# Gates made ahead and kept in DRAM, and up-projections moved past a triangular solve, in a five-branch decoder trunk

## The chip, the cores and the metric

The kernel runs on one core of a Trainium2 chip. The metric is the device time of one execution in microseconds (us). Names of engines: PE is TensorE (its weight loads are PEld), DVE is VectorE, ACT is ScalarE, POOL is GpSimd, SP is SyncE, whose queue issues nearly all DMAs.

## What is computed

One layer: a normalised input, one combined projection, four causal token mixers and one cross-attention, each with an up-projection and a merge gate of its own, and an output projection. SEQ is 2048, D_MODEL 1024, a branch is 512 wide, and everything is float32.

```python
h = rms_norm(x, norm_g[l])
p = h @ w_in[l]
(ret_q, ..., mem_q, gates) = split_cols(p, IN_SIZES)
o_ret = retention_branch(ret_q, ret_k, ret_v, positions) * silu(ret_g)
...                                  # o_gla, o_ssd, o_rwkv, o_mem in the same way
g = sigmoid(gates).reshape(b, t, N_BRANCHES, d)
merged = g[:, :, 0] * (o_ret @ w_up_ret[l])
for i in range(1, N_BRANCHES):
    merged = merged + g[:, :, i] * (o_i @ w_up_i[l])   # gla, ssd, rwkv, mem
x = x + merged @ w_out[l]
```

The gates need only the projection of `h`, so a gate can be made at any time of its pass. An up-projection needs the output `o` of its branch.

## The kernel before

The sequence is worked through in four passes of 512 tokens (`run`, the loop over `sc`). A pass does its branches in the order mem, retention, RWKV-7, SSD, GLA. While a branch is worked on, the gates and up-projections of the branch before it are fed in as units of work.

**Units.** `gate_units` makes eight pairs for a branch: `gate(d)` multiplies the normalised input by one 128-column block of gate weights (`proj`: 24 matmuls of 512 columns, since each float32 product is made of three parts) and ACT takes the tanh of it into an SBUF tile; `up(d)` multiplies the branch's output by a block of up weights (`mm3`: 12 matmuls, 6 for mem), DVE adds 1 to the tanh and multiplies (`stt`, line 302), and POOL or DVE adds the product to `merged[d]` (L1382). `inter` puts a branch's units in the order g0 g1 u0 g2 u1 ... g7 u6 u7, and they go to the list `self.fq`. Every `self.fill(n)` in a branch takes n units off that list. How many at which place is written out in `K.FILL`.

**Around the change.** Retention uses 8 of mem's 16 units, so when RWKV begins the list holds 8 of mem, 16 of retention and 4 output gates of RWKV (`rw_g`). RWKV has three parts. `rwkv_prep` makes its inputs (DVE, ACT and POOL do most of it). `rwkv_sys` inverts 64 triangular blocks: DVE solves by 31 pairs of a multiply and a row sum (L1196 and L1198), transposes twice (L1201 and L1203), ACT and POOL copy (L1208), and then PE does eight short groups, `lower(i)` and `corner(i)`, with copies between them. `fill(12)` stands behind the solve's lines and `fill(3)` ahead of `lower(0)`, so 15 units stand ahead of it; `lower(0)` is moreover tied to come after the last of them (`after=self.last`). `rwkv_chain` is a recurrence of eight chunks, with 13 units left for it. GLA comes last: its eight gates run one after the other behind it, then its eight ups, each with a slice of the next pass's input (`xhat_units`).

**Order.** The program's order is not the issue order. Behind `start` a planner orders each engine's instructions, SP's DMAs among them, ahead of time: an instruction that the planner takes to be ready may be moved ahead of earlier ones that are not, and its idea of the time is its own. On the chip each engine then runs its list strictly in that order. SBUF tiles named `s` come from one pool of 42 (`NS`), gate weights from four buffers (`wt`), the accumulators `acc` are three PSUM banks. Weights are split into two parts in the first pass and kept in DRAM (`kw`); later passes load them from there, 1 MB for a gate and 512 KB for an up (256 KB for mem).

Of the kernel before, what the change touches and what calls it, by code (L numbers as in the profile page):

```python
# [17 lines left out]
P = 128  # L18
# [126 lines left out]
class K:  # L145
# [131 lines left out]
    def nm(self, s):  # L277
        self.n += 1
        return f"{s}_{self.n}"

    NS = 42

    FILL = {"mem": (2, 0, 2, 2, 1, 1, 3, 3), "ret": (1, 3, 0), "late": (0, 0, 0, 0), "sys": (12, 3), "chain":
            (2, 3, 2, 1, 1, 2, 4, 3), "norm": 0, "ssd": (6, 0, 3, 4, 4), "gla": (3, 1, 2, 3, 1), "eng": (0, 1,
# [876 lines left out]
    def rwkv_sys(self, AR, KB):  # L1161
# [69 lines left out]
        for i in range(4):  # L1231
            nxt = lower(i + 1) if i < 3 else None
            corner(i, *z)
            z = nxt
# [103 lines left out]
    def rwkv(self, sc):  # L1338
        sg = []
        g = [lambda p=p: sg.append(self.silu2(self.proj(f"rw_g{p}"))) for p in range(4)]  # L1340
        self.fq += g
        wa = self.shift(12)
        self.nc.scalar.activation(wa[0:64, :], wa[0:64, :], AF.Tanh)
        AR, KB, gC = self.rwkv_prep(wa, range(4))
        Tt = self.rwkv_sys(AR, KB)
        BV = self.rwkv_chain(AR, KB, gC, Tt)
        self.fill(99)

        self.misc(sc)
        self.bm = [self.conv(sc, 4 + g) for g in range(2)]  # L1350
        return self.rwkv_fin(sc, BV, sg)


    def gate_units(self, key, o, eng=None):
        nc = self.nc
        nk = BRK[key]
        first = self.merged is None
        if first:
            self.merged = [None] * KT
        merged = self.merged  # L1360
        us = []
        for d in range(KT):
            th = []

            def gate(d=d, th=th):
                g = self.proj(f"gate{8 * BR[key] + d}")
                t = self.s()
                self.act(t, g, AF.Tanh, scale=0.5)
                th.append(t)

            def up(d=d, th=th):
                w = self.load_w(("wu_" + key, d), nk)
                ps = self.ps("acc")
                self.mm3(ps, w, lambda k: o[k], nk)
                t = th[0]
                if first:
                    m = self.xp.tile([P, T], F32, tag=f"mg{d}", name=self.nm("mg"))
                    merged[d] = m
                    self.stt(m, t, 1.0, ps, ALU.add, ALU.mult)
                else:  # L1380
                    self.stt(t, t, 1.0, ps, ALU.add, ALU.mult)
                    (eng or self.pick({"ret": 0, "rwkv": 1, "ssd": 2, "gla": 3}[key])).tensor_tensor(  # L1382
                        merged[d], merged[d], t, ALU.add)

            us.append((gate, up))
        return us

    @staticmethod
    def inter(us):

        g, u = [a for a, _ in us], [b for _, b in us]
        out = g[:2]
        for i in range(len(us)):
            out.append(u[i])
# [132 lines left out]
    def run(self):  # L1527
        for sc in range(self.nsc):
            last = sc + 1 == self.nsc
            self.merged = None  # L1530
            o = self.mem(sc)
            self.fill(99)
            for key, nxt in (("mem", "ret"), ("ret", "rwkv"), ("rwkv", "ssd"), ("ssd", "gla")):
                us = self.gate_units(key, o)
                self.fq += self.inter(us)
                if nxt == "ssd" and not last:
# [6 lines left out]
            self.bg = []  # L1543
            us = self.gate_units("gla", o, self.nc.vector if last else None)
            for gate, _ in us:
                gate()
            if not last:
                self.xh, xu = self.xhat_units(sc + 1, rs[0])
            hl = []
            for k in range(KT):  # L1550
                if not last:
                    xu[k]()
                us[k][1]()
            for k in range(KT):
# [85 lines left out]
```

## Time and profile before

| | us |
|---|---|
| runs: median of three | 3657.2 |
| runs: lowest and highest | 3652.63, 3668.01 |
| the profiled execution: its own time | 3662.73 |
| the profiled execution: span from first to last instruction | 3660.9 |
| PE busy in that span | 3462.5 (95%) |
| DVE, ACT and POOL busy | 1981.0, 983.9, 898.7 |
| mean granted clock of PE, as a share of full speed | 0.963 |

The triangular solve of the four passes ends near 400, 1336, 2211 and 3088 us, so a pass takes some 877 us; the first one starts behind the setup and also splits the weights. Matmuls are pipelined, so a busy PE need not be PE at its peak; the step from one start to the next tells the pace. The granted clock has two levels, 1.0 (2.4 GHz) and 0.5 (1.2 GHz). In the views, a number in square brackets behind an instruction is the time that its engine stood idle ahead of it, and what ended that.

### The profile page before, as it was taken

The page shows a single profiled execution, that of the slowest core. Times are in us where ns is not written, and L with a number is a line of the kernel's source. Part 1 is how long each engine was busy: PE and PEld are TensorE (multiplying, and loading weights), DVE is VectorE, ACT ScalarE, POOL GpSimd, SP SyncE. Part 2 cuts the span into 40 slices and gives each one's busy share as a digit, 9 for nine tenths or more (in the row PEclk, how much of TensorE's full clock was granted, in tenths as well). Part 3 has the DMA queues.
Part 4 walks back from the last instruction along what each step waited for, and adds up shares of the span by engine and source line. Part 5 has one row for each costly group of instructions (what it writes and reads, how often), then busy time and mean ns, then how long its engine had stood idle before and what let it go on. Part 6 is the DMA issues. An engine that isn't in the chain of part 4 may idle for free.

```text
span 3660.9 us, 51745 instructions
## 1 busy us (share of the span) xinstructions
PE 3462.5 (95%) x20368; PEld 2770.1 (76%) x20368; DVE 1981.0 (54%) x3189; ACT 983.9 (27%) x1796; POOL 898.7 (25%) x919
## 2 busy tenths in 40 slices
PE   7988898999899999999999998999999998999998
PEld 5766667777778677888887776778887877778887
DVE  6377557644454865662353785664345377464243
ACT  4243224342321321322131221222122132131212
POOL 3556425455421410211101231021100132020110
PEclk8988899999999989999999998999999999999999
DMA  6655535676765543545565553345465554344555
GB/s 201 229 191 188 176 120 202 212 253 218 267 212 164 159 136 113 178 150 172 170 221 175 153 172 116 124 152 184 161 215 184 169 158 147 111 151 149 170 171 191
DMA packets 226531, 639.59 MB, mean 175 GB/s; under 512 B 25184, under 2 KB 46192, under 8 KB 226288
## 3 DMA queue, kind: packets, MB, share of 16 engines
q1 hardware_dynamic: 225856, 635.76, 52.3%
q8 instruction: 161, 2.64, 0.3%
q14 instruction: 82, 0.67, 0.1%
q10 hardware_dynamic: 432, 0.52, 0.0%
HBM read 486.76 MB, written 145.23 MB: 173 GB/s over the span
## 4 chain that ended last, share of the span: by engine, by line
PE 53%; DVE 15%; issue 2%; ACT 2%; DMA 2%; POOL 0%; SPq 0%; DVEq 0%; POOLq 0%; ACTq 0%
PE acc L305 42%; DVE s L302 6%; PE br L305 6%; PE y L305 4%; DVE s L299 3%; DVE blk L299 2%; DVE blk L1198 1%; ACT s L296 1%; PE br L317 1%; DMA wt<-kw 1%; DMA s<-vtd 1%; DVE s L329 0%; DMA s<-in_xT_dram 0%; ACT blk L1182 0%; DVE s L339 0%
## 5 line engine op out<-in xcount | busy, mean ns | idle before, releaser
L305 PE MATMUL acc<-xhi,wt 128*128 128x512 f32 x5632 | 1836.1, 400 | 47.1 <-DVE s L299 15.2
L305 PEld LDWEIGHTS acc<-xhi,wt 128*128 128x128 f32 x5632 | 1075.5, 192 | 297.2 <-ACT s L296 20.8
L305 PE MATMUL acc<-xlo,wt 128*128 128x512 f32 x2816 | 1123.5, 399 | 2.3 <-DVE xlo L1518 1.5
L305 PEld LDWEIGHTS acc<-xlo,wt 128*128 128x128 f32 x2816 | 540.1, 192 | 115.5 <-issue 3.0
L305 PE MATMUL acc<-s,wt 128*128 128x512 f32 (+1 forms) x2448 | 600.9, 395 | 15.5 <-ACT wt L378 7.6
L305 PEld LDWEIGHTS acc<-s,wt 128*128 128x128 f32 x2448 | 455.8, 191 | 115.4 <-ACT wt L378 14.3
L302 DVE SCALAR_TENSOR_TENSOR s<-s,acc 128x512 f32<-128x512 f32 x192 | 131.4, 684 | 630.0 <-PE acc L305 348.6
L379 POOL TENSOR_TENSOR wt<-wr,wt 128x512 fp32r<-128x512 f32 (+1 forms) x256 | 354.7, 1391 | 406.6 <-ACT wt L378 391.8
L302 DVE SCALAR_TENSOR_TENSOR s<-s,s 128x512 f32<-128x512 f32 (+1 forms) x458 | 361.1, 792 | 30.9 <-ACT s L296 18.8
L379 POOL TENSOR_TENSOR s<-s,s 128x512 fp32r<-128x512 f32 x120 | 159.2, 1335 | 887.3 <-ACT s L378 758.3
L296 ACT ACTIVATE s<-acc 128x512 f32<-128x512 f32 x232 | 136.8, 596 | 725.1 <-PE acc L305 723.8
L1382 POOL TENSOR_TENSOR mg<-mg,s 128x512 f32<-128x512 f32 x64 | 87.4, 1366 | 576.5 <-DVE s L302 576.2
L378 ACT CAST wt<-wr 128x512 fp32r<-128x512 f32 (+1 forms) x256 | 155.5, 611 | 268.3 <-PE acc L305 132.9
L305 PE MATMUL br<-s,s 64*64 64x64 f32 (+6 forms) x2432 | 213.2, 279 | 15.2 <-DMA s<-vtd 4.8
L305 PEld LDWEIGHTS br<-s,s 64*64 64x64 f32 (+3 forms) x2432 | 165.1, 167 | 67.7 <-issue 40.8
L296 ACT ACTIVATE s<-s 128x512 f32<-128x512 f32 (+1 forms) x204 | 119.3, 610 | 298.6 <-DVE s L299 121.9
L378 ACT CAST s<-s 128x512 fp32r<-128x512 f32 x182 | 112.8, 620 | 300.9 <-DVE s L302 270.7
L299 DVE TENSOR_TENSOR s<-s 128x512 f32<-128x512 f32 (+1 forms) x167 | 149.2, 898 | 6.1
L305 PE MATMUL y<-s,s 128*64 128x64 f32 (+4 forms) x2112 | 138.0, 255 | 9.2 <-DVE s L299 6.7
L305 PEld LDWEIGHTS y<-s,s 128*64 128x64 f32 (+2 forms) x2112 | 113.5, 152 | 39.8 <-DVE s L299 12.5
L299 DVE TENSOR_TENSOR s<-s,s 128x512 f32<-128x512 f32 (+2 forms) x154 | 118.2, 793 | 41.2 <-ACT s L296 39.7
L317 PE MATMUL br<-cst,s 128*128 128x128 f32 x484 | 82.9, 296 | 49.5 <-DVE s L302 38.1
(218 smaller groups left out, 3247.3 us busy)
## 6 DMA issues: line engine op xcount, KB each, us to landing
wt<-kw SPq DMA_DIRECT2D x712, 512.0 KB, 3.3
kw<-wt SPq DMA_DIRECT2D x240, 512.0 KB, 3.1
wr<-in_wg_dram SPq DMA_DIRECT2D x176, 256.0 KB, 3.8
s<-in_xT_dram SPq DMA_DIRECT2D x88, 256.0 KB, 4.9
out_dram<-s SPq DMA_DIRECT2D x24, 256.0 KB, 2.5
wt<-kw SPq DMA_DIRECT2D x24, 256.0 KB, 3.1
s<-s SPq DMA_DIRECT2D x64, 64.0 KB, 2.0
bvd<-s SPq DMA_DIRECT2D x16, 256.0 KB, 2.6
```

The source lines that it names most:

```text
L296: self.nc.scalar.activation(out, in_, f, bias=bias, scale=scale, **kw)
L299: self.nc.vector.tensor_tensor(out, a, b, op)
L302: self.nc.vector.scalar_tensor_tensor(out, a, s, b, op0, op1)
L305: i = self.nc.tensor.matmul(out, lhsT=lhsT, rhs=rhs, start=start, stop=stop)
L317: self.nc.tensor.transpose(out, in_, self.c["ident"])
L378: self.nc.scalar.copy(hi, src)
L379: (eng or self.nc.gpsimd).tensor_tensor(lo, src, hi.bitcast(F32), ALU.subtract)
L1198: nc.vector.tensor_reduce(X[:, s_, s_ + 1:], pv, AX.X, ALU.add)
L1382: (eng or self.pick({"ret": 0, "rwkv": 1, "ssd": 2, "gla": 3}[key])).tensor_tensor(merged[d], merged[d], t, ALU.add)
```

## The change

The gates of all branches but mem become units of their own (`gates` with `far=True`): the tanh is stored to a DRAM tile as soon as it is made, and `up(d)` loads it again, the load for `up(d + 1)` being issued in `up(d)` (and the one for d = 0 there as well). Five gates (`EARLY`) of RWKV, SSD and GLA join the list of the branch before; three stay in the list of their own. Of retention all eight gates go to the list ahead of RWKV, and its ups, with the four output gates, are held back (`self.later`) until `rwkv_sys` has been written out. The counts in `rwkv_sys` become 9 and 2, and one unit is put between `lower(i + 1)` and `corner(i)`, four times. The last GLA stage makes three gates ahead of its ups instead of eight. The number of matmuls and of tanhs is the same as before.

```diff
--- before.py
+++ after.py
@@ -279,8 +279,9 @@
         return f"{s}_{self.n}"
 
     NS = 42
-
-    FILL = {"mem": (2, 0, 2, 2, 1, 1, 3, 3), "ret": (1, 3, 0), "late": (0, 0, 0, 0), "sys": (12, 3), "chain":
+    EARLY = 5
+
+    FILL = {"mem": (2, 0, 2, 2, 1, 1, 3, 3), "ret": (1, 3, 0), "late": (0, 0, 0, 0), "sys": (9, 2, 1), "chain":
             (2, 3, 2, 1, 1, 2, 4, 3), "norm": 0, "ssd": (6, 0, 3, 4, 4), "gla": (3, 1, 2, 3, 1), "eng": (0, 1,
             0, 1, 0, 1, 0, 0, 1, 1, 1, 1, 1), "rope": (3, 3)}
 
@@ -1230,6 +1231,7 @@
         z = lower(0, self.last)
         for i in range(4):
             nxt = lower(i + 1) if i < 3 else None
+            self.fill(K.FILL["sys"][2])
             corner(i, *z)
             z = nxt
         return Ab
@@ -1338,11 +1340,12 @@
     def rwkv(self, sc):
         sg = []
         g = [lambda p=p: sg.append(self.silu2(self.proj(f"rw_g{p}"))) for p in range(4)]
-        self.fq += g
+        self.later += g
         wa = self.shift(12)
         self.nc.scalar.activation(wa[0:64, :], wa[0:64, :], AF.Tanh)
         AR, KB, gC = self.rwkv_prep(wa, range(4))
         Tt = self.rwkv_sys(AR, KB)
+        self.fq += self.later
         BV = self.rwkv_chain(AR, KB, gC, Tt)
         self.fill(99)
 
@@ -1351,28 +1354,47 @@
         return self.rwkv_fin(sc, BV, sg)
 
 
-    def gate_units(self, key, o, eng=None):
-        nc = self.nc
+    def gates(self, key, far=False):
+
+        nc = self.nc
+        th = [None] * KT
+
+        def gate(d):
+            g = self.proj(f"gate{8 * BR[key] + d}")
+            t = self.s()
+            self.act(t, g, AF.Tanh, scale=0.5)
+            if far:
+                th[d] = self.dp.tile([P, T], F32, name=self.nm("gth"), tag=f"gth_{key}_{d}")
+                nc.sync.dma_start(th[d], t)
+            else:
+                th[d] = t
+
+        def get(d):
+            if far and d < KT:
+                t = self.s()
+                nc.sync.dma_start(t, th[d])
+                th[d] = t
+
+        return [lambda d=d: gate(d) for d in range(KT)], th, get
+
+    def ups(self, key, o, gates, eng=None):
+
         nk = BRK[key]
+        _, th, get = gates
         first = self.merged is None
         if first:
             self.merged = [None] * KT
         merged = self.merged
         us = []
         for d in range(KT):
-            th = []
-
-            def gate(d=d, th=th):
-                g = self.proj(f"gate{8 * BR[key] + d}")
-                t = self.s()
-                self.act(t, g, AF.Tanh, scale=0.5)
-                th.append(t)
-
-            def up(d=d, th=th):
+            def up(d=d):
+                if d == 0:
+                    get(0)
+                get(d + 1)
                 w = self.load_w(("wu_" + key, d), nk)
                 ps = self.ps("acc")
                 self.mm3(ps, w, lambda k: o[k], nk)
-                t = th[0]
+                t = th[d]
                 if first:
                     m = self.xp.tile([P, T], F32, tag=f"mg{d}", name=self.nm("mg"))
                     merged[d] = m
@@ -1382,15 +1404,14 @@
                     (eng or self.pick({"ret": 0, "rwkv": 1, "ssd": 2, "gla": 3}[key])).tensor_tensor(
                         merged[d], merged[d], t, ALU.add)
 
-            us.append((gate, up))
+            us.append(up)
         return us
 
     @staticmethod
-    def inter(us):
-
-        g, u = [a for a, _ in us], [b for _, b in us]
+    def inter(g, u):
+
         out = g[:2]
-        for i in range(len(us)):
+        for i in range(len(u)):
             out.append(u[i])
             out += g[i + 2:i + 3]
         return out
@@ -1530,9 +1551,20 @@
             self.merged = None
             o = self.mem(sc)
             self.fill(99)
+
+            G = {key: self.gates(key, key != "mem") for key in BR}
+            g = {key: G[key][0] for key in BR}
+            E = K.EARLY
             for key, nxt in (("mem", "ret"), ("ret", "rwkv"), ("rwkv", "ssd"), ("ssd", "gla")):
-                us = self.gate_units(key, o)
-                self.fq += self.inter(us)
+                us = self.ups(key, o, G[key])
+                if key == "mem":
+                    self.fq += self.inter(g[key], us)
+                elif key == "ret":
+
+                    self.fq += g[key] + g[nxt][:E]
+                    self.later = us
+                else:
+                    self.fq += self.inter(g[key][E:] + g[nxt][:E], us)
                 if nxt == "ssd" and not last:
                     rs, self.bg = self.xhat_stats(self.xsrc(sc + 1), T)
                 o = getattr(self, nxt)(sc)
@@ -1541,16 +1573,16 @@
             for u in self.bg:
                 u()
             self.bg = []
-            us = self.gate_units("gla", o, self.nc.vector if last else None)
-            for gate, _ in us:
-                gate()
+            us = self.ups("gla", o, G["gla"], self.nc.vector if last else None)
+            for u in g["gla"][E:]:
+                u()
             if not last:
                 self.xh, xu = self.xhat_units(sc + 1, rs[0])
             hl = []
             for k in range(KT):
                 if not last:
                     xu[k]()
-                us[k][1]()
+                us[k]()
             for k in range(KT):
                 hl.append(self.half_split(self.merged[k]))
             self.fq = self.out_units(sc, hl, last)
```

## Rows read from the trace of the kernel before

**Rows 1.** The page's head and its first part: span, and busy time, share and instructions of each engine.

```profile
span 3660.9 us, 51745 instructions
...
PE 3462.5 (95%) x20368; PEld 2770.1 (76%) x20368; DVE 1981.0 (54%) x3189; ACT 983.9 (27%) x1796; POOL 898.7 (25%) x919
```

**Rows 2.** Busy time by stretch of the third pass: the triangular solve, the recurrence, and the end of GLA with its gates and ups. Columns: the stretch and its length, then for each engine busy us and instructions, then the granted clock, the DMA engines' busy share and GB/s.

```profile
2167.00:2211.00 44.00, 38.87 (x171) 31.48 (x169) 42.07 (x67) 2.40 (x4) 3.31 (x2) 1.00 0.63 202
...
2229.00:2347.00 118.00, 115.26 (x1154) 87.74 (x1154) 54.27 (x109) 21.30 (x42) 6.38 (x5) 0.96 0.32 107
...
2642.00:2743.00 101.00, 100.22 (x470) 82.56 (x470) 41.88 (x64) 20.20 (x35) 7.79 (x6) 1.00 0.63 209
```

**Rows 3.** PE's waits around the solve, asked for three stretches: the first pass (340 to 430), the second (1285 to 1345) and the third (2160 to 2225). Columns: who waits, for whom, us in total, times, longest.

```profile
PE br L305 <- DVE blk L1203: 5.5, 1, 5.5
...
PE br L305 <- DVE blk L1203: 4.9, 1, 4.9
...
PE br L305 <- DVE blk L1203: 6.5, 1, 6.5
PE acc L305 <- DVE s L302: 2.1, 1, 2.1
```

**Rows 4.** DVE in order of time at the end of the third pass's solve: start, us, operation. L302 with `acc` is the add-and-multiply of an up; L299 and L1198 on `blk` are the solve; L1201 and L1203 its transposes.

```profile
2198.76 0.68 DVE L302 SCALAR_TENSOR_TENSOR s<-s,acc 128x512 f32<-128x512 f32 x1
...
2207.80 1.80 DVE L299 TENSOR_TENSOR blk<-blk,blk 128x961 f32<-128x961 f32 x1
2209.52 0.68 DVE L302 SCALAR_TENSOR_TENSOR s<-s,acc 128x512 f32<-128x512 f32 x1
2210.11 1.14 DVE L1198 TENSOR_REDUCE blk<-blk 128x31 f32<-128x961 f32 x1
2211.29 1.90 DVE L1201 STREAM_TRANSPOSE blk<-blk 128x1024 f32<-128x1024 f32 x1
2213.11 1.20 DVE L1203 STREAM_TRANSPOSE blk<-blk 128x1024 f32<-128x1024 f32 x1
2214.24 0.65 DVE L302 SCALAR_TENSOR_TENSOR s<-s,acc 128x512 f32<-128x512 f32 x1
```

**Rows 5.** PE in order of time in the same place. `acc<-s,wt` x12 is an up, `acc<-xhi,wt` and `acc<-xlo,wt` belong to gates, `br<-blk,s` is `lower`, `br<-s,zs` is `corner`.

```profile
2186.33 2.88 PE L305 MATMUL acc<-s,wt 128*128 128x512 f32 x12
...
2194.49 2.88 PE L305 MATMUL acc<-s,wt 128*128 128x512 f32 x12
2199.49 0.50 PE L305 MATMUL acc<-xhi,wt 128*128 128x512 f32 x1 [2.12 <-DVE s L302]
...
2205.11 2.88 PE L305 MATMUL acc<-s,wt 128*128 128x512 f32 x12
2214.46 2.91 PE L305 MATMUL br<-blk,s 32*32 32x32 f32 x96 [6.48 <-DVE blk L1203]
2217.31 0.80 PE L305 MATMUL acc<-xhi,wt 128*128 128x512 f32 x1
...
2224.74 1.06 PE L305 MATMUL br<-s,zs 32*32 32x32 f32 x32
...
2239.42 1.75 PE L305 MATMUL acc<-s,wt 128*128 128x512 f32 x7
```

**Rows 6.** PE in order of time ahead of the solve: an up of mem (its six matmuls), two groups of the recurrence's first chunk (`y`, lines that stand behind the whole of `rwkv_sys` in the program), and the products that the solve works on (`br<-s,s` x128).

```profile
2143.59 1.52 PE L305 MATMUL acc<-s,wt 128*128 128x512 f32 x6
...
2153.34 0.71 PE L305 MATMUL y<-Srw,s 64*64 64x64 f32 x16
...
2157.61 3.95 PE L305 MATMUL br<-s,s 64*64 64x64 f32 x128
```

**Rows 7.** Busy time by stretch, columns as in rows 2: the end of the solve, `lower` and `corner`, the first chunk of the recurrence, and, from retention's start in the same pass, a run of dense matmuls behind an idle time of PE.

```profile
2205.00:2214.40 9.40, 2.99 (x14) 2.13 (x12) 9.30 (x8) 1.11 (x2) 2.28 (x3) 0.86 0.77 249
2214.40:2229.00 14.60, 14.54 (x282) 12.35 (x282) 7.34 (x15) 7.54 (x17) 5.22 (x8) 0.50 0.02 4
2229.00:2240.00 11.00, 11.00 (x86) 7.89 (x86) 1.94 (x5) 1.53 (x4) 0.00 (x0) 0.70 0.13 48
...
1949.60:1958.30 8.70, 8.64 (x25) 6.85 (x26) 1.21 (x4) 0.00 (x0) 1.27 (x1) 0.65 0.70 236
```

**Rows 8.** Busy time by stretch, columns as in rows 2: GLA's eight gates in the third pass, its eight ups behind them, and the eight ups of the last pass.

```profile
2665.00:2709.00 44.00, 43.84 (x194) 35.98 (x193) 14.74 (x21) 5.10 (x9) 2.70 (x2) 1.00 0.58 191
2709.00:2731.00 22.00, 22.00 (x99) 18.23 (x98) 18.35 (x30) 6.11 (x11) 0.00 (x0) 1.00 0.82 286
...
3586.00:3608.00 22.00, 22.00 (x99) 18.22 (x98) 14.14 (x22) 4.42 (x7) 0.00 (x0) 1.00 0.93 326
```

**Rows 9.** DMA issues of the whole span: what, how many, KB each, median us from issue to landing.

```profile
wt<-kw SPq DMA_DIRECT2D x712, 512.0 KB, 3.3
...
s<-in_xT_dram SPq DMA_DIRECT2D x88, 256.0 KB, 4.9
...
bvd<-s SPq DMA_DIRECT2D x16, 256.0 KB, 2.6
```

**Rows 10.** SP's queue in order of time in the third pass's recurrence (the second column runs from the first issue of a run to the end of its last), and PE's wait for such a load in that stretch (2216 to 2347).

```profile
2303.95 11.46 SPq L434 DMA_DIRECT2D wt<-kw  x4
2315.46 0.45 SPq L1253 DMA_DIRECT2D s<-vtd  x1
...
PE br L305 <- DMA s<-vtd: 1.7, 2, 1.4
```

## The prediction

> **What bounds the kernel now.** First the page's busy times: PE is busy for 95% of the span and DVE, the next, for 54% [rows 1]. The change leaves the number of matmuls as it is, so time can only come from what PE loses: idle time and half clock. Next the pace: 36 matmuls of an up and a gate start within 8.16 us, 0.2267 us each [rows 5]. Against that pace I went through the third pass stage by stage. GLA's end, from which the change takes gates, has almost nothing to give: PE is busy 100.22 of 101 us at full clock [rows 2]. The recurrence is busy 115.26 of 118 us [rows 2]; its loss is in short matmuls taking turns with long ones, which more filling doesn't cure. What is left is the solve. Ahead of `lower(0)` PE stands idle 5.5, 4.9 and 6.5 us in three passes [rows 3], I take 6 in all four, and then works at half clock through `lower` and `corner` [rows 7]. That place is what the change can win or lose.
>
> **The cover ahead of lower(0).** Before, 15 units stand ahead of it: u3 g5 u4 g6 u5 g7 u6 u7 of mem (5 x 6 + 3 x 24 = 102 matmuls), then g0 g1 u0 g2 u1 g3 u2 of retention (4 x 24 + 3 x 12 = 132), 234 in all. After, there are 11: the same 102 and three gates, 174. The 60 that go are 13.6 us of cover. On the other side, DVE does two of the ups' multiplies between the steps of the solve at 0.68 us each [rows 4]; without them the solve ends 1.3 us sooner. PE's wait of 2.1 us for such a multiply [rows 3] goes as well, but PE then only reaches the end of the solve sooner, so that is worth nothing.
>
> How much of the 13.6 us is made good? The planner moves ready work up: an up of mem is done ahead of the products that the solve needs, and so are two groups of the recurrence from behind the whole of `rwkv_sys` [rows 6]. A fourth gate and more are ready in the same way. It will fill until it believes the solve done. What it believes stands in DVE's list: u1's multiply lies between the last multiply and the last row sum [rows 4], so by its account u1 ended there. From there the solve needs at least 1.14 + 1.90 + 1.20 = 4.2 us, with the 0.68 and part of the 1.80 before it at most 6.7; say 5.5. PE had g3 and u2 ahead, 36 matmuls, 8.2 us. So before, being tied to u2, `lower(0)` was put some 2.7 us behind the moment at which the planner took the solve for done; in truth PE was still early by 6.5 us, as DVE ran u1's multiply at 2209.52 though u1's matmuls were over by 2199.49 [rows 4, 5]. After, `lower(0)` is tied to gate 2, which is over long before, so it goes where the planner sees the solve end: 2.7 us of cover less, and 1.3 us more through the earlier end on both sides, which cancels. I take 2.5 us of further idle time a pass, **+10 us** for four. Bounds a pass: -6 (the idle time closes) and +12.3 (nothing is moved up: 13.6 - 1.3).
>
> **The clock behind it.** From 2214.4 to 2229 PE ran at 0.50 of its clock and to 2240 at 0.70 [rows 7]: at most 14.6 x 0.50 + 11 x 0.30 = 10.6 us of full speed. Most of it isn't the clock's, as `lower` and `corner` wait for copies. After, with `fill(1)` ahead of `corner`, two gates or so stand ahead of the last corners; behind an idle time, dense matmuls ran 8.7 us at 0.65 [rows 7], 3.0 us of full speed lost. So at most 7.6 us a pass come back, at least none. Part of the four gates will have been used up ahead of `lower(0)`, so I take the lower end, 2 us: **-8 us**.
>
> **The ups of GLA.** 32 gates a pass go through DRAM, not five of eight: all of retention, RWKV, SSD and GLA. That is 128 stores and 128 loads of 256 KB, 67 MB. For most branches gates and ups take turns and PE has slack for it. In GLA's end the eight ups follow each other: 22 us at 286 GB/s with the DMA engines busy 0.82, and in the last pass 326 GB/s at 0.93 [rows 8], so full use is some 350 GB/s. Eight loads more are 2.1 MB: (6.3 + 2.1) MB at 350 GB/s is 24.0 us, 2.0 over the 22; in the last pass (7.2 + 2.1) gives 26.6, 4.6 over. Some loads will be issued during the gates ahead, at 0.58 busy [rows 8], so I take 2 a pass: **+8 us**, bounds 0 and +11. The Trainium skill's page "DMA: Bandwidth & Descriptors", section "Specifications", speaks against this part of the change as well: it gives about 358 GB/s as what one core gets of HBM. The highest stretch here, 326 GB/s, stays under that; by the page's figure the overruns would be an estimated 1.4 and 4.0 us instead of 2.0 and 4.6.
>
> **SP's queue and DVE's.** Each store waits on SP for its tanh, and whatever is queued there waits behind it: weight loads first. A weight load takes 3.3 us to land and a load of 256 KB 2.6 to 4.9 [rows 9], and four weight buffers are two gates (10.9 us) of lead, so a wait of a microsecond is hidden; if that cover is gone, a store costs its wait in full. The gates' loads have no such lead: one up, 2.7 us, ahead. In the recurrence SP already sat 11.46 us on weight loads ahead of a chunk's values, for which PE waited 1.7 us [rows 10]; the gates' loads join that queue, and a late one holds up DVE, which the next chunk needs. I take half a microsecond a pass: **+2 us**, bounds 0 and +9 (one load of 4.9 us seen in each pass less the 2.7 us of lead, four passes). Everything else costs nothing: tanhs, multiplies and adds are as many as before, and 27 us of gates (5 x 24 x 0.2267) leave GLA's end and turn up in the solve and the recurrence, on PE both times.
>
> **Sum.** +10 - 8 + 8 + 2 = +12 us on the profiled execution's 3662.7, or 3675. That execution lies 5.5 us above the median, so against the median 3657.2 + 12 = **3669 us**, no change within what a measurement here can tell (0.5%, 18 us).
>
> **Rivals.** *PE never runs dry.* Gates need nothing of DVE, so if the planner puts enough of them ahead of `lower(0)`, the 6 us of idle time go (-24 for four) and with them the fall of the clock, of whose 10.6 us I count half (-21). For it: the four gates placed there by name. Against it: 6.5 + 2.7 us more of them, 40 matmuls, would have to be moved up than the planner has reason to [rows 4, 5]. It gives 3657 - 45 = 3612 with the loads hidden, and 3622 with them. The Trainium skill's page "TensorE: Matmul & The Clock Gate", section "Why this matters for your kernels", asks for bursts without idle time between, so that the clock stays up. The trace agrees as far as it goes: the clock was low behind the idle 6.48 us [rows 5, 7]. *The cover is simply gone.* If nothing is moved up past `lower(0)`, each pass loses 12.3 us: 49 for four, and 3657 + 49 = 3706. It decides from about 11 us of idle time there, 4.5 more than now. Against it: work was moved up past it before [rows 6]. *The loads are late everywhere.* One load seen in full in each branch and pass, 4.9 - 2.7 us, 16 times, is 35, on top of the 12: 3704.
>
> **How the numbers follow.** Forecast 0.40, PE never dry 0.30, cover gone 0.17, loads late 0.13. So faster by over 0.5% 0.30, within 0.40, slower 0.30. Of the forecast itself the bounds are 3645 to 3690; the range takes in most of both sides: 3612 to 3708.
>
> **What would show it.** Right: the wait of `lower(0)` for L1203 at 8 to 10 us; gates of retention beyond the third ahead of it; DMA above 0.9 in GLA's ups with PE no longer gapless; no waits of PE on `wt` elsewhere. Wrong: that wait gone and the clock at 1.0 through `lower` (rival one); a wait of 15 us or more (rival two); DVE's multiplies waiting for DMA in SSD and GLA (rival three). What I can't see is the planner's own times; if it takes gates for longer than they are, it moves fewer of them up.

## The result, and the profile after

The changed kernel takes 3701.2 us (median of 4 runs, 3699.7 to 3702.63), the kernel before 3658.81 in the same rounds: a ratio of 1.0122, 95% interval 1.0102 to 1.0141, so some 45 us slower. That lies in the predicted range, but the forecast itself, +12 us and no change that can be measured, isn't what came.

The page of the changed kernel, head and PE's row. As many matmuls as in [rows 1], PE busy 4 us less, the span 40 us longer: the loss is idle time of PE. (Lines of the code come one to some twenty numbers later than before: L305 is now L306, L1203 is L1204, L1253 is L1255.)

```profile
span 3700.8 us, 52293 instructions
...
PE 3458.7 (93%) x20368; PEld 2760.2 (75%) x20368; DVE 1992.6 (54%) x3189; ACT 984.1 (27%) x1796; POOL 891.4 (24%) x919
```

Busy time by stretch of the third pass, columns as in [rows 2]: the solve, the recurrence, and GLA's end, which is 21 us shorter as its gates went elsewhere.

```profile
2182.00:2226.00 44.00, 34.83 (x154) 28.52 (x152) 41.97 (x67) 3.60 (x6) 0.03 (x1) 0.92 0.63 193
2257.00:2380.00 123.00, 117.27 (x1168) 89.17 (x1167) 59.78 (x114) 19.63 (x39) 11.40 (x8) 0.99 0.47 146
2691.00:2771.00 80.00, 75.24 (x353) 61.49 (x353) 42.15 (x64) 17.43 (x30) 7.85 (x6) 0.98 0.72 242
```

Against [rows 2] PE does 4 us less in the 44 of the solve; in the recurrence its idle time went from 2.7 to 5.7 us and its clock from 0.96 to 0.99; GLA's end, gapless before, has 4.8 us of gaps. The same views, cut at the same instructions in all four passes (the solve's first and last transposes, the last copy of `corner`, the last chunk's copy of Y, GLA's last mask, the next pass's first reduction), give these sums. Idle is the length of a stretch less PE's busy time, clock is the length times what the granted clock lacks to 1:

| us in four passes | idle before | idle after | clock before | clock after |
|---|---|---|---|---|
| solve, up to its end | 24.6 | 42.4 | 5.0 | 15.3 (nearly all while PE is idle) |
| from there to the last corner | 15.0 | 12.7 | 28.0 | 29.1 |
| recurrence | 14.6 | 30.1 | 24.7 | 9.0 |
| GLA's end | 22.3 | 30.0 | 7.9 | 13.3 |

Idle time grew by 38.7 us; the clock gives 14.6 back between the solve's end and the end of the recurrence, and takes 5.4 in GLA's end. That is 30 of the 40 us; the other 10 I did not place. Over the whole span PE's idle time (span less busy time) went from 198.4 to 242.1 us, so 5 us of it lie outside these stretches. What the clock lacks is not all time: PE's busy time as a whole fell by 3.8 us only.

PE's waits in the whole span, the three that grew most. The second fence has the first two for the kernel before.

```profile
PE br L306 <- DVE blk L1204: 50.8, 4, 13.3
...
PE br L306 <- DMA s<-vtd: 17.9, 15, 2.3
...
PE acc L306 <- DMA wt<-kw: 12.5, 8, 4.5
```

```profile
PE br L305 <- DVE blk L1203: 23.4, 4, 6.5
...
PE br L305 <- DMA s<-vtd: 4.8, 7, 1.6
```

**Place one, `lower(0)`.** DVE and PE in order of time at the end of the third pass's solve, to be laid beside [rows 4, 5]:

```profile
2223.17 1.78 DVE L300 TENSOR_TENSOR blk<-blk,blk 128x961 f32<-128x961 f32 x1
2224.99 1.15 DVE L1199 TENSOR_REDUCE blk<-blk 128x31 f32<-128x961 f32 x1
2226.18 1.90 DVE L1202 STREAM_TRANSPOSE blk<-blk 128x1024 f32<-128x1024 f32 x1
2228.00 1.20 DVE L1204 STREAM_TRANSPOSE blk<-blk 128x1024 f32<-128x1024 f32 x1
```

```profile
2216.44 0.39 PE L306 MATMUL acc<-xhi,wt 128*128 128x512 f32 x1
2229.35 2.91 PE L306 MATMUL br<-blk,s 32*32 32x32 f32 x96 [12.52 <-DVE blk L1204]
```

No multiply of an up stands between the solve's steps any more, and PE has nothing to do for 12.52 us. Busy time behind it, columns as in [rows 7]:

```profile
2217.00:2229.00 12.00, 0.00 (x0) 0.00 (x0) 11.76 (x9) 0.82 (x2) 0.73 (x2) 0.58 0.18 54
2229.40:2244.00 14.60, 14.60 (x215) 11.68 (x216) 3.39 (x8) 5.85 (x12) 3.73 (x7) 0.54 0.18 56
2244.00:2255.00 11.00, 11.00 (x121) 8.85 (x119) 0.00 (x0) 2.65 (x6) 0.00 (x0) 1.00 0.69 184
```

The first 14.6 us run at half clock as before (0.54, before 0.50), the next 11 at full clock (before 0.70).

**Place two, GLA's end.** Busy time of the ups, then PE's row with the gap, then SP's queue ahead of it in order of time (second column: from a run's first issue to the end of its last):

```profile
2736.00:2758.00 22.00, 17.49 (x71) 14.02 (x70) 19.96 (x32) 7.96 (x14) 0.00 (x0) 0.92 0.92 336
```

```profile
2743.99 15.47 PE L306 MATMUL acc<-s,wt 128*128 128x512 f32 x60 [4.51 <-DMA wt<-kw]
```

```profile
2713.58 14.83 SPq L435 DMA_DIRECT2D wt<-kw  x6
2731.00 1.31 SPq L1368 DMA_DIRECT2D gth<-s  x3
2732.36 0.46 SPq L508 DMA_DIRECT2D s<-in_xT_dram  x1
2732.86 0.94 SPq L1375 DMA_DIRECT2D s<-gth  x2
...
2737.10 0.42 SPq L435 DMA_DIRECT2D wt<-kw  x1
```

Between two weight loads SP issues three stores of gates, and then, in turns, the next pass's input and the gates that are wanted back: no weight is asked for from 2728.4 to 2737.1. PE does its first three ups and then stands for 4.51 us. The weight it stands for also came late: asked for at 2737.10, used from 2743.99, where the median landing is 3.6 us. In the kernel before, the same queue had eight weight loads up to 2709.41 and its next one 2.5 us later:

```profile
2690.05 19.36 SPq L434 DMA_DIRECT2D wt<-kw  x8
2709.46 2.32 SPq L507 DMA_DIRECT2D s<-in_xT_dram  x5
2711.88 0.38 SPq L434 DMA_DIRECT2D wt<-kw  x1
```

**Place three, the recurrence**: the 17.9 us for a chunk's values. DMA issues of the whole span, columns as in [rows 9]: the trip is 128 stores and 128 loads, and weights land 0.3 us later than before.

```profile
wt<-kw SPq DMA_DIRECT2D x712, 512.0 KB, 3.6
...
gth<-s SPq DMA_DIRECT2D x128, 256.0 KB, 3.9
s<-gth SPq DMA_DIRECT2D x128, 256.0 KB, 4.4
```

### The profile page after: what moved, and what is told of

Its sections match the earlier page's. It is cut to its first block, busy times and chain, and to the rows that moved or that the text cites. A ratio compares the mean times of both kernels' runs of the same rounds, so it can differ in the third digit from the quotient of the medians.

```text
span 3700.8 us, 52293 instructions
## 1 busy us (share of the span) xinstructions
PE 3458.7 (93%) x20368; PEld 2760.2 (75%) x20368; DVE 1992.6 (54%) x3189; ACT 984.1 (27%) x1796; POOL 891.4 (24%) x919
## 4 chain that ended last, share of the span: by engine, by line
PE 47%; DVE 15%; DMA 5%; ACT 3%; issue 2%; SPq 1%; POOL 0%; DVEq 0%; ACTq 0%; POOLq 0%
PE acc L306 37%; DVE s L303 6%; PE br L306 5%; PE y L306 4%; DVE s L300 3%; DVE blk L300 2%; DMA wt<-kw 2%; ACT s L297 2%; DMA s<-vtd 1%; DVE blk L1199 1%; DMA s<-gth 1%; PE br L318 1%; DMA s<-in_xT_dram 1%; DVE s L330 0%; ACT blk L1183 0%
## 5 line engine op out<-in xcount | busy, mean ns | idle before, releaser
L306 PE MATMUL acc<-xhi,wt 128*128 128x512 f32 x5632 | 1826.9, 399 | 30.0 <-DVE s L300 15.1
L306 PEld LDWEIGHTS acc<-xhi,wt 128*128 128x128 f32 x5632 | 1071.9, 191 | 274.3 <-DVE s L300 17.5
L306 PE MATMUL acc<-xlo,wt 128*128 128x512 f32 x2816 | 1119.6, 398 | 2.5 <-DVE xlo L1539 1.8
L306 PE MATMUL acc<-s,wt 128*128 128x512 f32 (+1 forms) x2448 | 621.9, 402 | 33.9 <-ACT wt L379 10.1
L306 PEld LDWEIGHTS acc<-xlo,wt 128*128 128x128 f32 x2816 | 538.8, 191 | 115.7 <-DVE xlo L1539 3.0
L306 PEld LDWEIGHTS acc<-s,wt 128*128 128x128 f32 x2448 | 459.9, 194 | 140.6 <-ACT wt L379 17.1
L380 POOL TENSOR_TENSOR wt<-wr,wt 128x512 fp32r<-128x512 f32 (+1 forms) x256 | 347.0, 1360 | 424.1 <-ACT wt L379 396.7
L306 PE MATMUL br<-s,s 64*64 64x64 f32 (+6 forms) x2432 | 206.3, 273 | 29.7 <-DMA s<-vtd 17.9
L306 PEld LDWEIGHTS br<-s,s 64*64 64x64 f32 (+3 forms) x2432 | 159.8, 162 | 82.4 <-issue 38.9
L306 PE MATMUL y<-s,s 128*64 128x64 f32 (+4 forms) x2112 | 137.5, 254 | 8.7 <-DVE s L300 6.2
L306 PEld LDWEIGHTS y<-s,s 128*64 128x64 f32 (+2 forms) x2112 | 113.2, 152 | 38.0 <-DVE s L300 11.5
L306 PE MATMUL acc<-wt,xhi 128*128 128x512 f32 x384 | 120.8, 396 | 6.0 <-DVE s L303 4.0
```

The costliest lines, as they stand in the source:

```text
L306: i = self.nc.tensor.matmul(out, lhsT=lhsT, rhs=rhs, start=start, stop=stop)
L380: (eng or self.nc.gpsimd).tensor_tensor(lo, src, hi.bitcast(F32), ALU.subtract)
```

## The experiments

My theory was that the loss sits at these three places, each with a cause of its own; the rivals were that the traffic costs wherever it is, that the new order costs, or that work put into the solve is only missing in the recurrence. All ratios are to runs of the kernel before on the same chip; differences in us are differences of ratios times 3657.

**e1_cover: more gates ahead of `lower(0)`.**

```diff
-    FILL = {..., "sys": (9, 2, 1), ...
+    FILL = {..., "sys": (13, 2, 1), ...
```

> The changed kernel with four more gates put ahead of lower(0): the first entry of FILL['sys'] is 13 instead of 9, nothing else differs, and the sum of the work is the same. By the list of PE's instructions 57 more projection matmuls then stand ahead of the first lower than in the changed kernel, 57 x 0.2267 = 12.9 us, about what PE waits there (12.7 us a pass). Theory one (the missing cover ahead of lower(0) is what costs most): the wait of lower(0) for the end of the solve falls from 12.7 us a pass to under 2, the stretch at half clock behind it goes, and the time falls by 25 to 40 us from 3701, to 3661 to 3676. Rival (the work is only missing elsewhere): the recurrence, which now has four gates less, loses what the solve gains, and the time stays within 8 us of 3701.

1.0030 (1.0012 to 1.0048): 34 us less than the changed kernel. The wait for the end of the solve is 0.26 us in the third pass, PE's idle time in the solve's four stretches fell from 42.4 to 7.2 us, and the recurrence didn't lose what was gained (idle 23.8 for 30.1). The rival is out. The edit brought a new wait behind `lower(0)`: the idle time from there to the last corner went from 12.7 to 30.4 us in four passes. PE, ACT and SP there, in order of time, and SP's wait in 2195 to 2222:

```profile
2208.67 1.98 PE L306 MATMUL br<-blk,s 32*32 32x32 f32 x64 [0.26 <-DVE blk L1204]
2217.89 0.77 PE L306 MATMUL acc<-xhi,wt 128*128 128x512 f32 x1 [7.24 <-DMA wt<-kw]
```

```profile
2207.49 5.17 ACT L1209 COPY s<-blk 32x256 f32<-32x256 f32 x8 [14.75 <-DVE blk L1202]
2212.69 1.57 ACT L297 ACTIVATE s<-acc 128x512 f32<-128x512 f32 x3
```

```profile
2213.31 0.32 SPq L1368 DMA_DIRECT2D gth<-s  x1
2213.72 0.88 SPq L435 DMA_DIRECT2D wt<-kw  x2
```

```profile
SPq L1368 <- ACT s L297: 15.4, 1, 15.4
```

ACT stands for the solve with its copies, three tanhs stand behind these copies, a store stands on SP for the first of them, and two weight loads stand behind the store: PE goes without a weight for 7.24 us. The prediction had this chain ("a store costs its wait in full" if the cover of the weight buffers is gone) and gave it no price of its own.

**e2_glaend: GLA's loads written ahead of its last gates, and those three gates kept in SBUF.**

```diff
-            if far:
+            if far and (key != "gla" or d < K.EARLY):      # store
...
-            if far and d < KT:
+            if far and d < (K.EARLY if key == "gla" else KT) and d not in got:
+                got.add(d)
...
+            for d in range(E):
+                G["gla"][2](d)
             for u in g["gla"][E:]:
```

> The changed kernel with another end of GLA: its gates 5 to 7, which are made right ahead of the ups, stay in SBUF, and the five from DRAM are all asked for before these three gates are made, not one up ahead. Theory one (the loads of the gates are squeezed into the ups, where the weights then come late): PE's gap of about 4.5 us for a weight in the ups of passes two and three goes with the half clock behind it; the stage loses 5 to 6 us a pass less in passes one to three, so 10 to 16 us less in all, 3685 to 3691. Rival (the DMA engines are full over the whole end, whenever the loads are asked for): less than 5 us, 3696 or more.

1.0058 (1.0034 to 1.0082): 23 us less, with an uncertainty of some 11 us. Third pass's GLA end, columns as above:

```profile
2680.10:2755.20 75.10, 74.85 (x362) 61.31 (x362) 42.60 (x65) 17.21 (x30) 7.85 (x6) 1.00 0.70 239
```

As many matmuls (362) as the changed kernel has between its same two instructions in 81.2 us, now in 75.1, with no gap and no fall of the clock. Idle time of the four ends fell from 30.0 to 16.9 us, below the 22.3 of the kernel before. The rival (full whenever asked for) is out: the DMA engines moved 239 GB/s, hardly less than in the changed kernel (242). But two things differ here, three stores and three loads fewer in each end, and the order; e3_near3 parts them. And the loads are not where the program has them. The planner put eight weight loads ahead of them, and they went out in one run as the last gate ended (the ups begin at 2721.0), with the next weight right behind:

```profile
2718.44 2.32 SPq L1377 DMA_DIRECT2D s<-gth  x5
2720.86 0.38 SPq L435 DMA_DIRECT2D wt<-kw  x1
```

**e3_near3: gates 5 to 7 stay in SBUF.**

```diff
-            if far:
+            if far and d < K.EARLY:      # store
...
-            if far and d < KT:
+            if far and d < K.EARLY:      # load
```

> The changed kernel with gates 5 to 7 of the branches that go through DRAM left in SBUF (only the five that are made a branch ahead, and the first five of retention, are stored and loaded): 80 stores and 80 loads instead of 128 of each, 25 MB less, in the same order of work. Theory one (single late loads cost, in GLA's end and the recurrence, not the traffic as such): the loads of GLA's last three ups go, the last of a crunch that starts with the first: 3 to 8 us less, 3693 to 3698, and the wait of lower(0) stays at 12 to 13 us. Rival (the trip through DRAM costs in proportion to what is moved): three eighths of the 42 us that were lost, 16 us less, 3685.

1.0049 (1.0033 to 1.0065): 27 us less, far above what my theory said and above the rival's 16. The wait of `lower(0)` is unchanged (50.9 us in four passes). It decides nothing between the two but the price: gates that are made and used in one branch had no business in DRAM. It also prices GLA's end. The same 362 matmuls of the third pass take 76.6 us, with a gap of 1.37 us for a weight:

```profile
2663.00:2739.60 76.60, 74.93 (x362) 61.41 (x361) 42.51 (x65) 17.32 (x30) 7.81 (x6) 1.00 0.64 227
```

```profile
2716.66 3.68 PE L306 MATMUL acc<-s,wt 128*128 128x512 f32 x15 [1.37 <-DMA wt<-kw]
```

So of the 6.1 us that e2 won there (81.2 to 75.1), 4.6 come without its order, with the three stores and three loads that are gone. Whether these cost by their bytes or by their place on SP was not parted. Where the rest of e3's 27 us comes from was not followed.

**e4_trip: the order of before, with the trip through DRAM.**

```diff
-    EARLY = 5
-    FILL = {..., "sys": (9, 2, 1), ...
+    EARLY = 0
+    FILL = {..., "sys": (12, 3, 0), ...
...
-                    self.fq += g[key] + g[nxt][:E]
-                    self.later = us
+                    self.fq += self.inter(g[key], us)
+                    self.later = []
```

> The order of work of the kernel before (EARLY is 0, FILL['sys'] is 12, 3 and nothing ahead of the corners, retention's ups not held back), but all gates but mem's are stored to DRAM and loaded again, as in the changed kernel: the trip by itself. By the list of PE's instructions lower(0) then has the cover of before. Theory one: the wait of lower(0) is that of before (5 to 7 us a pass), the ups of GLA lose some 15 us to eight loads in each pass, and the recurrence some 5 to 7: 3675 to 3682. Rival one (the order costs, the trip is hidden): within 8 us of the kernel before. Rival two (the trip costs wherever it is): 3695 or more.

1.0090 (1.0060 to 1.0119), some 33 us slower than before (22 to 44): above my 18 to 25 but for the lower end of the interval. Rival one (the trip is hidden) is out; rival two (3695 or more, 38 us) is not. The profiled execution is one of the faster ones, only 16 us longer than that of before, so its waits show part of the loss. GLA's end has 30.6 us idle, as in the changed kernel, and the recurrence 20.3 (before 14.6). The wait of `lower(0)` went to 9.9 us, not to before's 23.4, because PE waits earlier instead: 38.2 us in all for DVE's multiplies on an up's products, 15.5 before; in the third pass 4.6 of it in the solve (2.1 in [rows 3]) and 3.4 in GLA's end. DVE in turn waits for gates from DRAM:

```profile
DVE s L303 <- DMA s<-gth: 103.5, 15, 33.8
```

That is the prediction's third sign, multiplies that wait for DMA; the change's own order takes most of it away (37.1 us in the changed kernel).

**e5_all: e1, e2 and e3 together.** The diffs are those above, with GLA's preloading and `d < K.EARLY` for every branch.

> The three edits so far in one kernel: 13 units ahead of lower(0) (e1_cover), only the gates that are made a branch ahead go through DRAM (e3_near3), and GLA's five are asked for ahead of its last three gates (e2_glaend). Theory one (the costs lie at separate places and add): the solve and the recurrence as in e1_cover, GLA's end as in e2_glaend, so some 23 us less than e1_cover, 10 us under the kernel before: a ratio to it of 0.993 to 0.999. Rival (e2_glaend and e3_near3 gain what e1_cover gained too, by less DMA traffic during the recurrence): no faster than e1_cover, a ratio of 1.000 to 1.004.

0.9937 (0.9922 to 0.9952): faster than the kernel before, and 34 us below e1_cover where I expected 23. Its three places: GLA's end as in e2, the solve as in e1, with the stall of 7 us still there (6.9 in the third pass).

**e6_nodram: retention's part alone, nothing a branch ahead, nothing in DRAM.**

```diff
-    EARLY = 5
-    FILL = {..., "sys": (9, 2, 1), ...
+    EARLY = 0
+    FILL = {..., "sys": (13, 2, 1), ...
...
-            G = {key: self.gates(key, key != "mem") for key in BR}
+            G = {key: self.gates(key) for key in BR}
...
-                    self.fq += g[key] + g[nxt][:E]
+                    self.fq += g[key]
```

> One part of the change without the other: nothing is made a branch ahead and nothing goes through DRAM (EARLY is 0, far is off for every branch), but retention's eight gates stand ahead of and within the systems (13, 2 and 1 units) and its up-projections come behind them. By the list of PE's instructions lower(0) has the cover of e1_cover. Theory one (putting gates there is what gains, the trip and the branch ahead only cost): solve and recurrence as in e1_cover, GLA's end as before; the kernel before with a wait of lower(0) of under 2 us instead of 6: 10 to 20 us under the kernel before, ratio 0.994 to 0.997. Rival (the gates made ahead are what lets the recurrence run well in e1_cover, since there is then more left to fill it with): the recurrence loses as in the kernel before, 96 us, and the ratio is 0.998 to 1.003.

0.9955 (0.9940 to 0.9970), 16 us faster than before, as expected. PE's idle time in the solve is 7.2 us in four passes, before 24.6, and from there to the end of the recurrence the clock lacks 28.8 us for 52.7. Retention's part of the change, its eight gates ahead of its ups, carries this gain and needs only SBUF. Against e1_cover (1.0030), which has the same cover, the trip and gates a branch ahead, that is 27 us, within e4's interval of 22 to 44: the price of the trip, if gates a branch ahead neither gain nor cost by themselves. That isn't shown: e5_all has them and a cheaper trip, and its interval meets e6's. PE's wait for a chunk's values is 1.8 us here, 15.1 in e1_cover and 12.7 in e4_trip (before 4.8): it comes with the trip, in either order of work.

**e7_vtdq: the chunk values on ACT's queue.**

```diff
-            nc.sync.dma_start(UV[0:64], self.vtd[...
+            nc.scalar.dma_start(UV[0:64], self.vtd[...
```

> The changed kernel with the loads of a chunk's values issued from ACT's queue instead of SP's, nothing else differs. Theory one (in the recurrence these loads stand on SP behind weight loads, which wait there for PE to free a buffer, 90 us in one recurrence, and behind the gates' loads; PE's 17.9 us of waiting for them is the queue): that wait falls under 5 us and the time by 8 to 15 us, to 3686 to 3693. Rival (they are late because the DMA engines carry more): the wait stays above 12 us and the time within 4 us of 3701.

A miss, and not a small one: 1.0195 (1.0178 to 1.0212), 27 us slower than the changed kernel, with PE's wait for these loads up from 17.9 us.

```profile
PE br L306 <- DMA s<-vtd: 25.2, 12, 3.1
```

Another queue is no cure. That does not clear the place in the queue, since the planner put the first of these loads behind the copies of `corner` on ACT too:

```profile
2266.38 0.36 ACT L1228 COPY s<-br 32x256 f32<-32x256 f32 x1
2266.39 0.45 ACTq L1255 DMA_DIRECT2D s<-vtd  x1
```

The wait is 7 us of the loss. The profiled span is 20.4 us longer, 12.6 of them PE's busy time, at a mean clock of 0.958 for 0.964; why the clock fell was not followed.

**e8_uvown and e11_ns44: buffers.** A chunk's values are loaded into one of 42 shared buffers. e8 gives them two of their own, e11 only makes the shared ones 44.

```diff
-            UV = self.s((P, 8, 64))
+            UV = self.s((P, 8, 64), tag="uv", bufs=2)      # e8
...
-    NS = 42
+    NS = 44                                                # e11
```

> The changed kernel with two buffers of their own for a chunk's values (tag uv) besides the 42 that everything else shares, so that such a load no longer waits for a shared buffer to come free. e7_vtdq has shown that SP's queue isn't why these loads are late. Theory one (it is the buffers: with the gates' tanhs and their copies from DRAM in the shared 42, one comes free late): PE's wait for the chunk values falls from 17.9 us to under 5, the recurrence loses 6 to 12 us less in all, and the time is 3689 to 3697. Rival (the loads land late because of the traffic, 4.0 us in the median and up to 6.9 us instead of 3.5): the wait stays above 12 us, the time within 4 us of 3701.

> The changed kernel with 44 shared buffers instead of 42 and none of its own for the chunk values: the control for e8_uvown. If e8_uvown gains by the buffers as such, this gains as much; if it gains because the chunk values' loads no longer queue for one, this stays within 4 us of 3701 and PE's wait for them above 12 us.

e8 is 1.0077 (1.0058 to 1.0096), 16 us less than the changed kernel, and PE's wait for these loads is gone from the list of its waits (all below 5 us in four passes). e11 is 1.0126 (1.0110 to 1.0142), no change, with 15.7 us of that wait. So it is not the number of buffers; what the two of their own change is where the loads stand on SP. SP's row and the landing times in e8:

```profile
2165.72 1.73 SPq L1255 DMA_DIRECT2D uv<-vtd  x2
```

```profile
DMA to landing us min/median/max: 2.2/2.6/4.4
```

The first two chunks' loads go out ahead of the third pass's solve, 77 us before the last corner of the same kernel at 2243.1 (in the changed kernel the first went out at 2256.0, behind the last corner), and they land in 2.6 us in the median, for 4.0 (both figures include the 16 stores of the values). The recurrence's idle time is 18.8 us in four passes, after 30.1. SP's waits at these loads in the whole span, the changed kernel and then e8:

```profile
SPq L1255 <- DVE s L303: 0.4, 2, 0.3
SPq L1255 <- DVE s L300: 0.2, 1, 0.2
```

```profile
SPq L1255 <- PE y L306: 43.0, 23, 5.8
SPq L1255 <- DVE uv L1291: 38.6, 13, 4.3
```

In the changed kernel SP hardly ever stands at such a load for its buffer, 0.6 us in all: it gets to the load late, behind weight loads that wait for PE (90.5 us in one recurrence). In e8 it gets there early and stands over 80 us for the two buffers. That the planner lists these loads late because it sees no shared buffer free in time is what I take from e8 and e11; the planner's own times are not shown. That the loads also land later under the trip's traffic was not parted from this, since an early load hides both.

**e9_all12 and e10_alluv: e5_all with one gate less of cover, and with e8's buffers.**

```diff
-"sys": (13, 2, 1)
+"sys": (12, 2, 1)                                     # e9
...
+            UV = self.s((P, 8, 64), tag="uv", bufs=2)  # e10
```

> e5_all with 12 instead of 13 units ahead of lower(0), so one gate, 24 matmuls or 5.4 us, less cover. In e1_cover and e5_all the stretch from the end of the solve to the last corner lost 3 us a pass more than in the changed kernel, as if lower(0) came some 3 us too late there. Theory one (cover costs what it is missing and what it is too much, both by the matmul): the wait of lower(0) is back with 2 to 3 us a pass, the stretch behind gives back some 3 us a pass, and the time is within 6 us of e5_all. Rival (any idle time there brings the half clock back): 15 to 25 us above e5_all.

> e5_all with the two buffers of e8_uvown. Theory one (buffers): PE's 14.0 us of waiting for the chunk values goes under 5 us, 5 to 12 us under e5_all. Rival (traffic): within 4 us of e5_all.

e9: 0.9913 (0.9896 to 0.9930), 9 us below e5_all, the intervals overlapping a little. The wait of `lower(0)` is back, with 5.4 to 6.2 us a pass instead of the 2 to 3 expected, and the 6.9 us for the late weight are gone. Neither theory had this trade. SP's store still waits 15.2 us for its tanh there; that PE, one gate less ahead, doesn't use up its weights meanwhile is what I take from it, not what was tried. e10: 0.9901 (0.9882 to 0.9921), 13 us below e5_all, as the theory of buffers said.

```profile
2173.02 2.01 PE L306 MATMUL br<-blk,s 32*32 32x32 f32 x64 [5.41 <-DVE blk L1204]
```

**e12_uv12: both.**

> e5_all with both last edits: 12 units ahead of lower(0) and two buffers of their own for the chunk values. Theory (solve and recurrence are separate places): the gains add, 0.9913 - (0.9937 - 0.9901), so a ratio of 0.986 to 0.990 to the kernel before, some 3605 us, with PE's wait of lower(0) at 5 to 6 us a pass and its wait for the chunk values under 2 us in all. Rival (what the 12 units gained in the stretch behind the solve is the same loss that the buffers take away): no faster than e10_alluv, 0.990.

0.9873 (0.9849 to 0.9896), 3604.0 us: the fastest of all, 46 us under the kernel before. The gains add. Idle time of PE in the order of the table above: 13.8, 15.4, 9.5 and 16.9 us. Page head, PE's row, and its wait of `lower(0)`:

```profile
span 3600.4 us, 52107 instructions
...
PE 3424.2 (95%) x20368; PEld 2745.7 (76%) x20368; DVE 1984.4 (55%) x3189; ACT 983.2 (27%) x1796; POOL 896.0 (25%) x919
```

```profile
PE br L306 <- DVE blk L1204: 22.3, 4, 6.1
```

That wait is as long as before (23.4). Of the 60.5 us between the two profiled spans, 38.3 are PE's busy time for as many matmuls, at a mean clock of 0.977 for 0.963, and 22.2 its idle time.

## Why the prediction was right or wrong

- **The time: in the range, by luck.** The range reached 3701 only because it took in two rivals, at 3706 and 3704 with 0.30 between them, and neither came as described. The forecast's own bounds, 3645 to 3690, were missed; they don't follow from the terms either, whose bounds add up to 3603 and 3726.
- **What bounds the kernel: right, but not where.** PE's work is the same and the loss is idle time, with the clock beside it. But "that place is what the change can win or lose" left out two places that lost 29 us. "GLA's end has almost nothing to give" is true only of what can be won: it lost 13 us. And "short matmuls taking turns with long ones" is not what the recurrence lost: of its 2.7 us idle in the third pass, PE waited 1.7 for the chunk values [rows 10] and 1.0 for DVE, and of the 24.7 us that its clock lacked, e12_uv12 has 3.7 left.
- **The cover ahead of `lower(0)`, +10 predicted, +18 measured: right in mechanism, too small.** Idle time in the solve went from 24.6 to 42.4 us. The planner did move gates up past the fixed 11 units: counted on PE's list, 21 matmuls fewer stand ahead of `lower(0)`, not 60. I had taken 2.7 us less cover a pass; 21 x 0.2267 is 4.8. The solve ended 1.2 us sooner (44.6 us from its first transpose to the next one, for 45.8; I had said 1.3), and the 2.1 us for an up's multiply moved into this wait, as said. 6.5 + 4.8 - 1.2 + 2.1 = 12.2 us; the row says 12.52. The wait came between my "8 to 10" and rival two's "15 or more"; it passed that rival's other mark, "about 11", though 39 of the 60 matmuls had been moved up. e1 shows that it is a matter of cover.
- **The clock, -8 predicted, -15 measured.** The two stretches behind the solve lack 38.1 us of clock for 52.7, all of it given back in the recurrence and none in `lower` and `corner`; how much time that gave is not shown, as PE's busy time in the whole span fell by 3.8 us. I took the lower end because gates would be used up ahead of `lower(0)`; fewer were.
- **GLA's ups, +8 predicted, +13 measured** (7.7 idle, 5.4 clock), above its bound of 11. I had priced eight loads at 350 GB/s, 2 us in each pass. The idle time comes to that sum by luck: by pass it is -1.0, 4.0, 4.0 and 0.8 us. I left out the three stores that go out right ahead of the ups: with them my estimate for the third pass would have been (6.3 + 2.9) MB at 350 GB/s, 26.2 us, 4.2 over the 22. And I had the half clock behind the gap at nothing, without a reason; the clock there lacks 5.4 us more than before. e2 and e3 show the place to be right; bytes and order are not parted.
- **SP's queue and the loads, +2 predicted, +15 measured** (idle time of the recurrence 14.6 to 30.1), above its bound of 9. **This step failed.** It allowed for one late load in each pass, at most 2.2 us, and for a delay by way of DVE. PE itself waited 15 times in four passes for a chunk's values, 1.2 us in the mean: 17.9 us, for 4.8 before. So the price of one late load was not too low, their number was. e8 lets these loads go out early and gains 16 us. (Of the "2.6 to 4.9" us for a load, 2.6 is a store's [rows 9].)
- **The rivals.** "PE never runs dry" is not what the change does, as it takes cover away; e6_nodram shows what it is worth. In e6 the idle time of the solve falls by 17 us and the clock's loss behind it by 24 (I had said 24 and 21), but the runs gain 16 us and the profiled execution 30, not 45. The difference of 30 and 16 is the choice of execution: the profiled one of before lies 11.5 us above the median of the runs beside e6 (3651.2), that of e6 2.0 under its own. And of the 24 us of clock, PE's busy time shows 10.2. "The cover is simply gone" fell by the planner's 39 matmuls. "Loads late everywhere" (+35 on top) came nearest in size: the trip costs some 27 to 33 us by e1 against e6 and by e4. It had the wrong places: not one load in each branch, but the recurrence and GLA's end.
- **The Trainium skill's figure.** In the sentence on the Trainium skill's page "DMA: Bandwidth & Descriptors", section "Specifications", I set 358 GB/s against GLA's ups. The ups of the changed kernel run at 336 GB/s over 22 us, below it, but see the last section.

**Still open:** DVE waits 70.1 us in four passes for RWKV's bonus values from DRAM (one wait of 17 to 18 us in each) in the changed kernel, and 69.3 in e5_all, for 7.1 before; whether PE pays for that was not tried. All gates kept in SBUF in the changed order was not tried either, since I took the 42 buffers not to suffice.

## What to carry to other kernels

A buffer in DRAM isn't free storage. Here 128 tiles stored and loaded again cost some 33 us, and each step of the trip has to be looked at by itself: what stands behind a store that waits on the issuing queue (7.24 us of PE in e1_cover), what else the DMA engines carry in that stretch (GLA's end), and which loads of others come late by it (17.9 us of PE in the recurrence). A load that a chain of dependent steps waits for deserves buffers of its own, so that it can be asked for early; two of them were worth 16 us, while two more shared ones were worth nothing. And where a planner fills a gap, count what is fixed ahead of the gap against its true length: four units more ahead of `lower(0)` took back 34 of the 45 us.

## What was not expected of the hardware

The DMA engines went above what I had called full use, 350 GB/s. Two stretches of GLA's end in the changed kernel, columns as above:

```profile
2739.00:2747.00 8.00, 3.49 (x11) 2.51 (x10) 7.23 (x13) 2.47 (x4) 0.00 (x0) 0.84 1.04 401
2740.00:2755.00 15.00, 11.01 (x42) 8.98 (x43) 13.46 (x22) 4.66 (x8) 0.00 (x0) 0.89 0.94 368
```

368 GB/s over 15 us and 401 over 8, with one core at work. A busy share of 1.04 says that a window of 8 us is short for this view, so the 368 is the firmer figure. The Trainium skill's page "DMA: Bandwidth & Descriptors", section "Specifications", gives about 358 GB/s as the limit of one core, as half of what two cores share; here the measurement decides.
